# A hybrid decoder layer on one core: squares of two norms summed through PSUM, and a convolution's edge terms on ScalarE

## The chip, the cores and the metric

The kernel runs on one core of a Trainium2 chip. Five engines work beside each other, each on its own queue in order: TensorE (PE; its weight loads are listed apart as PEld), VectorE (DVE), ScalarE (ACT), GpSimd (POOL) and SyncE (SP), which issues most of the DMAs here. The engines work on tiles in SBUF; products land in PSUM, which has eight banks of 128 partitions by 512 floats. The metric is the time of one execution on the device, in microseconds (us).

## The reference, cut to what matters

One decoder layer over a sequence of 1024 positions with 1024 channels, all in float32. Three mixers (a state-space scan, stick-breaking attention, sparse attention) give `mixed`; then comes what the change touches:

```python
def rms_norm(x, w):
    xf = x.astype(jnp.float32)
    y = xf * lax.rsqrt(jnp.mean(xf * xf, axis=-1, keepdims=True) + NORM_EPS)
    return (y * w.astype(jnp.float32)).astype(x.dtype)
...
x = x + rms_norm(mixed @ w_out[l], post_mix_norm[l])
h = rms_norm(x, pre_ffn_norm[l])
u = causal_dwconv(h @ ffn_w_up[l], ffn_conv_w[l], ffn_conv_b[l])
gate, val = jnp.split(u, 2, axis=-1)
f = (jax.nn.gelu(gate, approximate=True) * val) @ ffn_w_down[l]
x = x + rms_norm(f, post_ffn_norm[l])
```

So there is an output projection with a norm behind it, a residual, a second norm, a projection up to 2 x 2816 channels, a causal convolution of three taps along the sequence for each channel, a gate, and a projection down. The convolution of a position needs the two positions before it.

## The kernel before, in words

Tiles are feature major: 128 channels lie on the partitions and 512 positions, half of the sequence, along the free axis. `h` is 0 or 1 for the half. A weight of 128 output channels is one unit. Every product is made of three passes in a reduced format: `load_w` (L263) loads a weight (`wraw`), ACT copies its rounded part (`whi`, L268) and POOL subtracts to get the rest (`wlo`, L269); the input has `hi` and `lo` in the same way, and a product of 128 inputs is hi*hi, hi*lo and lo*hi, recorded at L204. Two buffers hold each of `wraw`, `whi` and `wlo`, so the next weight's split runs while TensorE works on this one.

`tail_stage` (L1199) holds the part around the change. It takes the eight PSUM banks in two pools: `psd` for products (tile `dense`) and `psn` for the norms.

- The output projection runs half by half. For each of eight units, ACT copies the product into `o[j]` (L1303) and `sumsq` squares it with a second activation into an SBUF tile `osq` (L1281), and DVE adds the squares into the first of them (L1285). `rstd` multiplies the sum by a matrix of ones on TensorE, which sums over the partitions, and makes the reciprocal root out of it with DVE and ACT (L1292 to L1297), as a `psn` tile. This product is in full float32, and takes two passes on TensorE.
- Then for each of the eight tiles of the half: scale by the norm (L1310), add the residual `ox` (L1312), square and sum again (L1281, L1285), and write the tile out. `O_POOL` names the tiles, 0 and 2, whose residual addition and whose sum POOL does; these two squares make a sum of their own, so that the second `rstd` has two products with ones to add.
- The second norm scales the tiles (L1318) and splits them into `hi` (ACT, L1321) and `lo` (DVE L1327, or POOL L1325). These are the inputs `h2` of the FFN.
- The first four pairs of FFN units (`N_FIRST`) are computed half by half (`up_half`, L1406). Unit by unit, `conv` (L299) convolves the product: ACT makes the first tap with the bias (L302), DVE keeps the last two columns of the first half (`halo`, L304), adds the shifted taps (L306), and for the second half adds the first columns' terms from the halo (L308). The gate unit goes through Gelu on ACT (L1400), and `gated` multiplies (L1403).
- The other 18 pairs are computed by `up_pair` (L1413): seven products in place of eight from sums and differences of quarters of the weights (`weights7`, L1337: `uf` on POOL L1354 to L1356 and L1359, `uhi` on ACT L1357 and L1360) and of `h2` (`combos`, L1384). Three banks x, y and z of `psd` are in use for a pair; ACT takes copies of partial results (`snap`, L1381), and DVE combines banks and copies (L1421, L1433) before the convolution. One pair is 84 passes on TensorE.
- The down projection (`down`) follows, adding into `acc` in SBUF (L1493), and a last norm.

What order the instructions of an engine have isn't the order of the program: a planner with a simulated time line places them when the program is built, and only calls marked by `keep_in_program_order` stay where they are written. So a change of a few instructions' engines or tiles can reorder others near them. A tile is reused once its readers are done.

## Time and profile before

| what | us |
|---|---|
| median of three runs | 2301.05 (2300.88 to 2301.59) |
| profiled execution | 2302.9 |
| its span | 2300.9 |
| TensorE busy | 2212.4 (96%) |
| VectorE busy | 1399.1 (61%) |
| ScalarE busy | 1126.5 (49%) |
| GpSimd busy | 1112.6 (48%) |

In the profile a row is a group of instructions: line, engine, operation, the tile written and the tiles read, shapes and count, then busy time, mean duration in ns, and the idle time of the engine ahead of them with what ended it. The chain of waits is followed back from the last instruction; it names for each step the work that released the next. The windows give the busy time of the engines in a stretch of the span, and the granted clock of TensorE as a fraction of full speed. In timeline rows the bracket holds the idle time of the engine ahead of the instruction and the instruction that ended it.

### The profile page before, as it was taken

How to read it: one execution, taken by the hardware profiler on the slowest of the kernel's cores; microseconds unless marked ns; L12 is line 12 of the kernel's file. 1: busy time of each engine (PE TensorE's matmuls, PEld its weight loads, DVE VectorE, ACT ScalarE, POOL GpSimd, SP SyncE). 2: the span in 40 equal slices, each digit the busy share in tenths (PEclk: the TensorE clock that was granted, in tenths of full speed). 3: DMA queues.
4: the chain of work that ended last, by engine and by line, in shares of the span. 5: the costliest groups of instructions: out<-in, count | busy, mean ns of one | idle time of the engine just before them, and what ended most of it. 6: DMA issues, size and time to landing. Idle time of an engine off the chain costs nothing.

```text
span 2300.9 us, 29584 instructions
## 1 busy us (share of the span) xinstructions
PE 2212.4 (96%) x10804; PEld 1785.6 (78%) x10804; DVE 1399.1 (61%) x2419; ACT 1126.5 (49%) x1966; POOL 1112.6 (48%) x797
## 2 busy tenths in 40 slices
PE   8999998999999999999999999999899999999997
PEld 7997666667887878887777788887678888878886
DVE  8325784882377667647474543349977777753346
ACT  7144565666466666444444321245545555553224
POOL 4122565566233332635444336446578888822213
PEclk9999999999999999999999999999999999999998
DMA  5223112201111111111212164245322222264312
GB/s 197 80 84 99 53 37 68 65 5 44 47 46 49 48 51 37 65 65 55 74 46 97 68 223 135 94 143 175 107 90 83 83 83 83 83 222 134 93 32 74
DMA packets 102834, 196.57 MB, mean 85 GB/s; under 512 B 26721, under 2 KB 40737, under 8 KB 102689
## 3 DMA queue, kind: packets, MB, share of 16 engines
q1 hardware_dynamic: 102400, 194.47, 25.7%
q8 instruction: 85, 1.39, 0.2%
q14 instruction: 61, 0.49, 0.1%
q10 hardware_dynamic: 288, 0.22, 0.0%
HBM read 150.09 MB, written 44.56 MB: 85 GB/s over the span
## 4 chain that ended last, share of the span: by engine, by line
PE 77%; DVE 15%; issue 3%; ACT 3%; POOL 1%; DMA 1%; SPq 0%; DVEq 0%; ACTq 0%; POOLq 0%
PE dense L204 60%; PE ps_s L204 6%; PE ps_o L204 4%; PE ps_t L204 4%; PE ps_b L204 2%; DVE mx L812 2%; DVE u L306 1%; DVE row L306 1%; DVE x L1312 1%; DVE osq L1285 1%; DMA wraw<-in_wdn 0%; DVE x L1553 0%; POOL wlo L269 0%; DVE x L1465 0%; POOL R L1115 0%
## 5 line engine op out<-in xcount | busy, mean ns | idle before, releaser
L269 POOL TENSOR_TENSOR wlo<-wraw,whi 128x1024 fp32r<-128x1024 f32 (+2 forms) x158 | 327.1, 2071 | 526.1 <-ACT whi L268 516.6
L204 PE MATMUL dense<-h_hi,whi 128*128 128x512 f32 x992 | 401.4, 405 | 3.5 <-DVE row L306 3.4
L204 PE MATMUL dense<-h_lo,whi 128*128 128x512 f32 x992 | 392.9, 396 | 0.0
L204 PE MATMUL dense<-h_hi,wlo 128*128 128x512 f32 x992 | 391.4, 395 | 0.0
L268 ACT ACTIVATE whi<-wraw 128x1024 fp32r<-128x1024 f32 (+2 forms) x158 | 141.4, 895 | 316.9 <-PE dense L204 279.4
L204 PE MATMUL dense<-hi,whi 128*128 128x512 f32 x688 | 268.9, 391 | 3.9 <-ACT whi L268 3.9
L204 PE MATMUL dense<-hi,wlo 128*128 128x512 f32 x688 | 264.4, 394 | 7.1 <-POOL wlo L269 6.5
L204 PE MATMUL dense<-lo,whi 128*128 128x512 f32 x688 | 268.5, 390 | 0.7 <-POOL lo L1325 0.5
L204 PEld LDWEIGHTS dense<-h_hi,whi 128*128 128x128 f32 x992 | 188.1, 190 | 44.5 <-ACT sa L1025 3.6
L204 PEld LDWEIGHTS dense<-h_hi,wlo 128*128 128x128 f32 x992 | 187.5, 189 | 40.2 <-issue 1.1
L204 PEld LDWEIGHTS dense<-h_lo,whi 128*128 128x128 f32 x992 | 188.2, 190 | 36.1 <-issue 1.8
L852 POOL TENSOR_TENSOR wT_lo<-wT,wT_hi 128x512 fp32r<-128x512 f32 x132 | 169.2, 1291 | 90.0 <-ACT wT_hi L851 80.8
L204 PEld LDWEIGHTS dense<-hi,wlo 128*128 128x128 f32 x688 | 129.5, 188 | 36.8 <-POOL wlo L269 8.7
L204 PEld LDWEIGHTS dense<-hi,whi 128*128 128x128 f32 x688 | 129.6, 188 | 33.5 <-ACT whi L268 5.9
L204 PEld LDWEIGHTS dense<-lo,whi 128*128 128x128 f32 x688 | 129.6, 188 | 28.9 <-POOL lo L1325 1.4
L1042 POOL TENSOR_TENSOR s_lo<-sa,s_hi 128x512 fp32r<-128x512 f32 (+2 forms) x48 | 53.7, 1122 | 149.2 <-ACT s_hi L1041 137.8
L204 PE MATMUL dense<-x,uhi 128*128 128x512 f32 x360 | 117.1, 390 | 2.4 <-ACT uhi L1357 1.3
L841 ACT ACTIVATE wT<-ps_s 128x512 f32<-128x512 f32 x132 | 78.5, 594 | 71.1 <-PE ps_s L204 66.4
L306 DVE SCALAR_TENSOR_TENSOR u<-dense,pv,u 128x510 f32<-128x510 f32 (+1 forms) x140 | 101.9, 737 | 6.5 <-ACT u L302 6.4
L812 DVE TENSOR_REDUCE mx<-ps_t 128x1 f32<-128x384 f32 (+3 forms) x192 | 94.0, 514 | 18.8 <-PE ps_t L204 16.7
L1493 DVE TENSOR_TENSOR x<-x,dense 128x512 f32<-128x512 f32 x64 | 43.9, 686 | 86.6 <-PE dense L204 86.6
L851 ACT ACTIVATE wT_hi<-wT 128x512 fp32r<-128x512 f32 x132 | 82.2, 629 | 13.9 <-POOL wT L843 12.1
(422 smaller groups left out, 5271.1 us busy)
## 6 DMA issues: line engine op xcount, KB each, us to landing
wraw<-in_wfm SPq DMA_DIRECT2D x62, 512.0 KB, 3.4
wraw<-in_wup SPq DMA_DIRECT2D x52, 512.0 KB, 3.4
g_d<-gate_e SPq DMA_DIRECT2D x48, 256.0 KB, 2.1
ge<-g_d SPq DMA_DIRECT2D x24, 512.0 KB, 3.8
m_d<-u SPq DMA_DIRECT2D x44, 256.0 KB, 2.0
u<-m_d SPq DMA_DIRECT2D x36, 256.0 KB, 4.3
wraw<-in_wo SPq DMA_DIRECT2D x16, 512.0 KB, 3.4
wraw<-in_wdn SPq DMA_DIRECT2D x32, 256.0 KB, 2.7
```

The source lines that it names most:

```text
L204: i = f(*a, **k)
L268: act(hi, raw, AF.Copy)
L269: (V if tiles else P).tensor_tensor(lo, raw, fl(hi), op=OP.subtract)
L306: V.scalar_tensor_tensor(o[:, d:], ps[:, :512 - d], taps[d], o[:, d:], op0=OP.mult, op1=OP.add)
L812: V.tensor_reduce(mx[:, h, a, n:n + 1], pm[:, :w], axis=AX, op=OP.max)
L841: act(w.rearrange("p h q -> p (h q)"), pz, AF.Exp)
L851: act(hi, wf, AF.Copy)
L852: P.tensor_tensor(lo, wf, fl(hi), op=OP.subtract)
L1042: (P if SB_SLO else V).tensor_tensor(s_lo[:, c0:], a[:, c0:], fl(s_hi[:, c0:]), op=OP.subtract)
L1285: eng.tensor_tensor(sums[0], sums[0], sq, op=OP.add)
L1312: e.tensor_tensor(o[j], o[j], x, op=OP.add)
L1493: end = V.tensor_tensor(a, a, ps, op=OP.add)
```

## The change

Four edits. `sumsq` writes the first square of a norm to an SBUF tile and each later one to a tile of the PSUM pool `psn`; DVE adds it from there. The pool `psn` has three banks in place of two, `psd` five in place of six, and `osq` two buffers in place of six. `O_POOL` is gone: DVE adds all eight residual tiles and all seven sums, and each norm has one product with ones. In the FFN's convolution the first columns of the second half are no longer added by DVE at L308: ACT adds them with three activations of one column (the halo column times the tap, with the output's own column as bias), which are written ahead of DVE's shifted taps. The other convolution, ahead of the scan, keeps its form.

```diff
--- before.py
+++ after.py
@@ -179,13 +179,12 @@
 
 W_BUFS = (3, 4, 4)
 U_BUFS = 4
-OSQ = 6
+OSQ = 2
 
 N_FIRST = 4
 
 SB_SLO = 1
 SB_WLO = 0
-O_POOL = (0, 2)
 H_POOL = (0, 1, 3, 5)
 T_POOL = (range(8), (0, 1, 2))
 
@@ -296,15 +295,19 @@
     def hs(h):
         return slice(h * 512, (h + 1) * 512)
 
-    def conv(o, h, ps, taps, bias, halo):
+    def conv(o, h, ps, taps, bias, halo, by_act=False):
 
         n = len(taps) - 1
         act(o, ps, AF.Identity, bias=bias, scale=taps[0])
+        if h == 1 and by_act:
+            for d in range(1, n + 1):
+                for t in range(d):
+                    act(o[:, t:t + 1], halo[:, n - d + t:n - d + t + 1], AF.Identity, bias=o[:, t:t + 1], scale=taps[d])
         if h == 0:
             V.tensor_copy(halo[:, :n], ps[:, 512 - n:])
         for d in range(1, n + 1):
             V.scalar_tensor_tensor(o[:, d:], ps[:, :512 - d], taps[d], o[:, d:], op0=OP.mult, op1=OP.add)
-            if h == 1:
+            if h == 1 and not by_act:
                 V.scalar_tensor_tensor(o[:, :d], halo[:, n - d:n], taps[d], o[:, :d], op0=OP.mult, op1=OP.add)
 
     st1 = ctx.enter_context(ExitStack())
@@ -1200,8 +1203,8 @@
     E = L(env)
     A, act, V, P, mm, tr, fl, pvc = E.A, E.act, E.V, E.P, E.mm, E.tr, E.fl, E.pvc
     load_w, fm_unit = E.load_w, E.fm_unit
-    psd = es.enter_context(tc.tile_pool(name="psd2", reuse_waits="tile", bufs=6, space=PSUM))
-    psn = es.enter_context(tc.tile_pool(name="psn", reuse_waits="tile", bufs=2, space=PSUM))
+    psd = es.enter_context(tc.tile_pool(name="psd2", reuse_waits="tile", bufs=5, space=PSUM))
+    psn = es.enter_context(tc.tile_pool(name="psn", reuse_waits="tile", bufs=3, space=PSUM))
     mp = es.enter_context(tc.tile_pool(name="mixed", reuse_waits="tile", bufs=1))
 
     def hi_t(dt=R32):
@@ -1275,19 +1278,20 @@
         o = [x_t(F32) for _ in range(8)]
         rows.append(o)
 
-        def sumsq(sums, src, eng=V):
-
-            sq = ow.tile([128, 512], F32, name="osq", bufs=OSQ)
-            act(sq, src, AF.Square)
+        def sumsq(sums, src):
+
             if sums[0] is None:
-                sums[0] = sq
+                sums[0] = ow.tile([128, 512], F32, name="osq", bufs=OSQ)
+                act(sums[0], src, AF.Square)
             else:
-                eng.tensor_tensor(sums[0], sums[0], sq, op=OP.add)
-
-        def rstd(*sums):
+                sq = psn.tile([128, 512], F32, name="psn", tag="psn")
+                act(sq, src, AF.Square)
+                V.tensor_tensor(sums[0], sums[0], sq, op=OP.add)
+
+        def rstd(ss):
+            ss, = ss
             ps = psn.tile([128, 512], F32, name="psn", tag="psn")
-            for n, (ss,) in enumerate(sums):
-                mm(ps, E.ones, ss, start=n == 0, stop=n == len(sums) - 1)
+            mm(ps, E.ones, ss, start=True, stop=True)
 
             V.tensor_scalar(ss, ps, 1.0 / DM, EPS, op0=OP.mult, op1=OP.add)
             act(ps, ps, AF.Ln, scale=1.0 / DM, bias=E.eps)
@@ -1303,16 +1307,15 @@
             act(o[j], ps, AF.Copy)
             sumsq(ss, ps)
         r = rstd(ss)
-        ss, st = [None], [None]
+        ss = [None]
         for j in range(8):
             x = ow.tile([128, 512], F32, name="ox", bufs=8)
             nc.sync.dma_start(x, A["xT"][j * 128:(j + 1) * 128, hs(h)])
             V.scalar_tensor_tensor(o[j], o[j], pvc(PV_PM, j), r, op0=OP.mult, op1=OP.mult)
-            e = P if j in O_POOL else V
-            e.tensor_tensor(o[j], o[j], x, op=OP.add)
-            sumsq(st if j in O_POOL else ss, o[j], e)
+            V.tensor_tensor(o[j], o[j], x, op=OP.add)
+            sumsq(ss, o[j])
             nc.sync.dma_start(E.x1_d[j * 128:(j + 1) * 128, hs(h)], o[j])
-        r = rstd(ss, st)
+        r = rstd(ss)
         for j in range(9):
             if j < 8:
                 i = V.scalar_tensor_tensor(o[j], o[j], pvc(PV_FFN, j), r, op0=OP.mult, op1=OP.mult)
@@ -1395,7 +1398,7 @@
         if h == 0:
             st["halo", s] = up_.tile([128, 4], F32, name="halo", bufs=12)
         st[s, h] = up_.tile([128, 512], F32, name=f"u{s}")
-        E.conv(st[s, h], h, ps, [pvc(PV_FW, 3 * u + 2 - d) for d in range(3)], pvc(PV_FB, u), st["halo", s])
+        E.conv(st[s, h], h, ps, [pvc(PV_FW, 3 * u + 2 - d) for d in range(3)], pvc(PV_FB, u), st["halo", s], True)
         if s == 0:
             act(st[0, h], st[0, h], AF.Gelu_apprx_tanh)
```

## The prediction

> **What bounds the kernel now.** I read the profile from the whole to the place. First the page: busy shares, then the chain that ended last.

> ```profile
> span 2300.9 us, 29584 instructions
> PE 2212.4 (96%) x10804; PEld 1785.6 (78%) x10804; DVE 1399.1 (61%) x2419; ACT 1126.5 (49%) x1966; POOL 1112.6 (48%) x797
> PE 77%; DVE 15%; issue 3%; ACT 3%; POOL 1%; DMA 1%; SPq 0%; DVEq 0%; ACTq 0%; POOLq 0%
> ```

> TensorE is busy 96% of the span. An edit that moves work between the other engines can gain only where TensorE stands still. Where that is, the chain of waits shows by its long unbroken pieces (start, length, work):

> ```profile
> 1301.81 237.31 PE dense L204 x1033
> 1539.12 0.87 PE psn L204 x2
> ...
> 1713.90 285.91 PE dense L204 x1260
> ...
> 2068.93 195.54 PE dense L204 x884
> ```

> Between 1301.8 and 1539.1 us, 1713.9 and 1999.8, and 2068.9 and 2264.5 no edit of DVE, ACT or POOL can gain; it can only lose. One matmul there takes 285.91/1260 = 0.227 us. The changed code runs from 1470 (the output projection) to 2000 (the end of the FFN's up projection), so its chances lie in 1540 to 1714. The windows of that stretch, and one over the FFN loop behind it:

> ```profile
> 1580.00:1600.00 20.00, 18.07 (x77) 14.27 (x77) 18.32 (x23) 11.70 (x17) 13.54 (x7) 1.00 0.35 111
> 1600.00:1620.00 20.00, 18.18 (x78) 14.07 (x77) 19.33 (x23) 9.36 (x15) 9.25 (x4) 1.00 0.58 193
> 1620.00:1640.00 20.00, 17.84 (x75) 13.49 (x74) 16.87 (x26) 15.41 (x21) 13.26 (x7) 1.00 0.37 131
> 1640.00:1660.00 20.00, 14.45 (x55) 10.89 (x54) 20.00 (x32) 9.52 (x15) 9.81 (x3) 0.83 0.20 66
> 1680.00:1700.00 20.00, 17.84 (x77) 13.80 (x76) 18.51 (x12) 10.88 (x17) 18.70 (x9) 1.00 0.19 62
> 1700.00:1720.00 20.00, 16.49 (x72) 13.02 (x71) 9.87 (x19) 9.54 (x14) 13.55 (x10) 1.00 0.25 92
> 1740.00:2000.00 260.00, 260.00 (x1149) 215.29 (x1148) 182.15 (x246) 133.72 (x191) 217.73 (x124) 1.00 0.24 83
> ```

> The columns are the window, its length, then busy time with instructions of TensorE, its weight loads, DVE, ACT and POOL, and the granted clock. TensorE's idle time in the six windows is 1.93 + 1.82 + 2.16 + 5.55 + 2.16 + 3.51 = 17.1 us; that is all the change could take out, 0.74% of the span. In the FFN loop TensorE has none, and DVE is busy 0.70, ACT 0.51, POOL 0.84 of the time. What TensorE waited for from 1500 to 1720:

> ```profile
> PE dense L204 <- POOL wlo L269: 6.3, 3, 4.1
> PE dense L204 <- ACT snap L1381: 3.5, 2, 2.0
> PE dense L204 <- ACT whi L268: 2.6, 3, 1.2
> PE psn L204 <- DVE osq L1285: 1.8, 1, 1.8
> PE dense L204 <- ACT uhi L1357: 1.3, 1, 1.3
> ```

> Only one wait, 1.8 us, is for the sums of squares (osq, L1285). The largest, wlo (L269), is POOL's half of a weight's split; the change doesn't touch it, but it moves the DVE work that holds POOL up:

> ```profile
> 1528.78 2.40 POOL L269 TENSOR_TENSOR wlo<-wraw,whi 128x1024 fp32r<-128x1024 f32 x1 [3.04 <-ACT whi L268]
> 1529.71 2.02 DVE L1285 TENSOR_TENSOR osq<-osq 128x512 f32<-128x512 f32 x1 [3.42 <-ACT osq L1281]
> 1581.75 0.50 PE L204 MATMUL dense<-hi,wlo 128*128 128x512 f32 x1 [1.71 <-POOL wlo L269]
> 1617.91 1.98 PE L204 MATMUL psn<-osq,ones 128*128 128x512 f32 x4 [1.82 <-DVE osq L1285]
> 1642.01 1.89 DVE L1386 TENSOR_TENSOR x<-x 128x512 f32<-128x512 f32 x3
> 1645.11 9.27 POOL L269 TENSOR_TENSOR wlo<-wraw,whi 128x1024 fp32r<-128x1024 f32 x2 [6.03 <-ACT whi L268]
> 1649.24 0.74 DVE L306 SCALAR_TENSOR_TENSOR u<-dense,pv,u 128x511 f32<-128x511 f32 x1
> 1651.58 0.79 PE L204 MATMUL dense<-hi,wlo 128*128 128x512 f32 x1 [4.15 <-POOL wlo L269]
> 1652.17 0.63 PE L204 MATMUL dense<-hi,whi 128*128 128x512 f32 x1
> 1652.60 0.63 PE L204 MATMUL dense<-lo,whi 128*128 128x512 f32 x1
> ```

> An osq sum with both operands in SBUF, issued 0.9 us into a wlo, ends at 1531.73, 0.55 after the wlo: it took 2.02 us. The other way round, two wlo's took 9.27 us from 1645.11 while DVE ran SBUF-only work without a break, against 2.40 each; the first came through only when DVE reached L306 at 1649.24, which reads PSUM. TensorE then stood 4.15 us, and the clock granted in that window was 0.83.

> **The change, part by part.** Prices:

> ```profile
> L1285 DVE TENSOR_TENSOR osq<-osq 128x512 f32<-128x512 f32 x24 | 34.5, 1437 | 29.5 <-ACT osq L1281 28.8
> L1312 DVE TENSOR_TENSOR x<-x,ox 128x512 f32<-128x512 f32 x12 | 14.8, 1287 | 0.0
> L1493 DVE TENSOR_TENSOR x<-x,dense 128x512 f32<-128x512 f32 x64 | 43.9, 686 | 86.6 <-PE dense L204 86.6
> L308 DVE SCALAR_TENSOR_TENSOR u<-halo,pv,u 128x1 f32<-128x1 f32 (+1 forms) x88 | 64.6, 734 | 0.0
> L302 ACT ACTIVATE u<-dense,pv 128x512 f32<-128x512 f32 x70 | 52.1, 769 | 21.8 <-DVE dense L1433 12.1 <-DVE dense L1421 9.1 <-PE dense L204 0.5
> L1381 ACT ACTIVATE snap<-dense 128x512 f32<-128x512 f32 x72 | 40.2, 584 | 2.8 <-PE dense L204 2.8
> L974 ACT ACTIVATE row<-dense 128x4 fp32r<-128x4 f32 x16 | 2.8, 172 | 4.9 <-DVE row L971 3.9 <-DVE row L975 0.9
> ```

> (1) Squares through PSUM. DVE's 24 sums of 1437 ns become 28 sums with one operand in PSUM, which I price like L1493, also DVE with one operand in PSUM: 0.69. DVE goes from 34.5 to 19.3 us, and these sums leave POOL's way. It hides almost wholly: in 1500 to 1540 TensorE doesn't wait. Only the four norms' chains can show it. POOL loses four x additions and two osq sums; DVE gains four additions at 1.29 (L1312), 5.2 us, which here lie between the two norms of a half, ahead of the sum the next norm needs.

> (2) One sum instead of two in the second norm. A ones product is two passes in the trace ("x4" for two products at 1617.91, 1.98 us). Two products go, one per half; the chain's "PE psn" at 1539.12 prices one product, two passes, at 0.87. TensorE: 2 × 0.87 = −1.7 us, since those passes stand among products that TensorE runs without a gap.

> (3) One PSUM bank less for the products (six to five), one more for squares. A pair of the FFN loop is 84 products, 19.05 us at 0.227. Following the banks through TensorE's order, a bank is written again at the earliest 29 products (6.6 us) after its last write, in place of 39 (8.8 us). What must be over by then is the subtraction and the convolution that read the bank. In the loop:

> ```profile
> 1771.35 0.70 DVE L1433 TENSOR_TENSOR dense<-dense,snap 128x512 f32<-128x512 f32 x1 [0.80 <-PE dense L204]
> ...
> 1774.44 0.74 DVE L306 SCALAR_TENSOR_TENSOR u<-dense,pv,u 128x510 f32<-128x510 f32 x1
> ```

> From z's last product to the last read of its bank, 1771.35 to 1775.18, are 3.8 us; 6.6 − 3.8 = 2.8 us are left. Cost nothing; if that cover is gone, each of 18 pairs pays what is over.

> (4) Convolution terms of the second half: 88 L308 of DVE (64.6 us) become 132 activations of one column. Lower bound 0.172 (L974); upper bound 0.172 plus what scale and bias from a tile add to a 512-wide copy, 0.769 − 0.584 = 0.185, so 0.36. I take 0.36, as these have both operands: 132 × 0.36 = 48 us for ACT, six per pair, 2.1 of 19.05 us; ACT would go from 0.51 to 0.62. Ends: 23 and 48 us of ACT. In the loop that is hidden by TensorE's gapless run. But the DVE terms of such a unit now start after ACT's third, about 1.1 us behind the Identity (L302), and DVE saves 0.73 twice: the release of the bank moves by about −0.4 us. Uncovered, it would cost up to 1.1 us on a pair.
> [...]

> **Where it shows.** I placed the instructions in the new order on each engine and carried the durations above forward from 1540. Changes of TensorE's time:
> - First half, 1540 to 1600. The eight x additions on DVE end about where they did; the second norm's sums end 2 us earlier (0.69 in place of stretched ones). But the norm's Exp now sits on ACT behind a weight copy and a square that wait for TensorE, so r comes 0.5 us later. The copies of the weights move ahead of the copies of h2, which takes out the 1.71 at 1581.75; the first two up units are interleaved in the new order, hold both weight buffers and wait again for 0.5 and 0.9. Net about −0.5.
> - Second half, 1600 to 1640. The 1.82 at 1617.91 goes. In its place one wlo is late by about 2.0, as its whi is queued on ACT behind a square, a table load and a Gelu. Net +0.2.
> - 1640 to 1660. DVE's run of SBUF-only work ahead of the first L306 grows from 13 instructions to 15 (0.6 us each, as they start in a row): wlo comes 1.2 later. Net +1.2.
> - 1660 to 1714. The L308 before the first pairs are gone from DVE: uhi 0.45, and the second snap, behind the Gelu behind DVE, some 0.9 earlier. Net −1.3.
> - The loop, the down projection and the tail: 0; the order of their products is the same but for bank reuse.

> Sum: −1.7 − 0.5 + 0.2 + 1.2 − 1.3 = −2.1 us. The profiled execution took 2302.9 (its span and 2.0 around it), 1.85 over the median of the three runs, 2301.05. So: 2302.9 − 2.1 = 2300.8 by its own measure, 2298.9 by the median's.

> The unknown ends: each of the four place terms is a difference of queue positions, and is at best its whole wait gone (1.9, 1.8, 4.15, 3.5), at worst as much again.

> **The rivals.**
> (a) The loop breaks (slower). The three column terms stand on ACT between the Identity and everything queued behind it, the next uhi and snap among them, and z's bank has 6.6 us to come free. For: ACT waits in order. Against: ACT is idle half of the loop. It decides when the release takes over 6.6 us. With 0.4 us on each of 18 pairs, 7.2: 2298.9 + 7.2 = 2306.
> (b) The waits of both norms and POOL's fall away (faster). If DVE no longer meets POOL, then 1.71, 1.82 and most of the 4.15 go, with the half-rate products behind it (eight at 0.43 by their starts, +0.2 each, 1.6): 1.7 + 1.9 + 1.8 + 3 + 1 = 9.4 at best, 2292. For: the stretched rows. Against: the SBUF-only run at 1641 to 1649 is the combos' (L1386 to L1388), which the change doesn't touch.
> (c) ACT's order turns against it (slower). More activations stand in a row ahead of whi, and a late whi makes wlo late. If the wlo wait of the second half is 4 in place of 2, with a drop of the clock as at 1651.58, +2 + 1.6, and the same once more in the first half: 2298.9 + 5 = 2304.
> The clock's price is in the rows after 1651.58: 0.43 between starts instead of 0.227. [...]
> (d) Nothing but the saved product: 2301.05 − 1.7 = 2299.4, inside the forecast's own range.

> **How the numbers follow.** A measurement of this kernel tells 0.2% (4.6 us) from no change. Forecast with (d), 2296.4 to 2303: 0.46. (b), 2290 to 2296.4: 0.30. (a) 0.10 and (c) 0.14, together 2303 to 2311. Nearly all of the forecast's case is within 0.2% (0.42 of 0.46, the rest 0.02 on either side); of (b) nine tenths (0.27) are faster by more, of (a) and (c) seven tenths (0.17) slower by more. So faster 0.29, slower 0.19, same 0.52. The range leaves out the best of (b) and the worst of (a): 2291.5 to 2306.5.

> **What would show it.** L1285 at 0.69, 28 times, with psn as an operand; psn products two rows per norm; the new activations at 0.17 to 0.36, 132 times; no L308 on u; a TensorE piece of about 286 us again in the chain (a broken one is rival a); the waits for wlo within 1640 to 1660 near 5.4 (near 1: rival b; a second above 3: rival c). I am wrong if the loop isn't gapless, if the 1.2 at 1651 has the other sign, or if stages ahead of 1500 or behind 2000 differ by over 2 us.

## The result and the profile after

The changed kernel takes 2305.65 us in the median of 17 executions (2300.04 to 2307.67), the kernel before 2300.88 beside it (2299.47 to 2302.76): a ratio of 1.0016, with a 95% interval of 1.0010 to 1.0023. It is slower: by 3.7 us by the ratio, by 4.8 between these medians. Forecast was 2298.9, 2.1 less than before; the time is inside the stated range (2291.5 to 2306.5) and inside 0.2%, but on the other side of no change.

From the page of the changed kernel, and the long pieces of its chain of waits:

```profile
span 2303.9 us, 29654 instructions
PE 2216.0 (96%) x10800; PEld 1790.1 (78%) x10800; DVE 1341.3 (58%) x2339; ACT 1163.6 (51%) x2098; POOL 1102.4 (48%) x791
PE 80%; DVE 12%; ACT 3%; issue 2%; POOL 2%; DMA 1%; DVEq 0%; ACTq 0%; POOLq 0%
```

```profile
1302.18 236.90 PE dense L203 x1033
...
1699.34 299.74 PE dense L203 x1314
...
2064.90 202.56 PE dense L203 x908
```

TensorE has four rows less (10800 for 10804: two products with ones) and is yet busy 3.6 us longer, 2216.0 for 2212.4. The FFN loop runs unbroken, up to 1999.08 us where it ended at 1999.81 before, so at that point the changed kernel is 0.7 us ahead. The groups of instructions show that the column terms (0.376 us) and the sums (0.684) cost what was forecast, 0.36 and 0.69; the residual additions came cheaper, 0.818 where 1.29 was taken:

```profile
L305 ACT ACTIVATE u<-halo,u,pv 128x1 f32<-128x1 f32 x132 | 43.4, 376 | 0.6
L1289 DVE TENSOR_TENSOR osq<-osq,psn 128x512 f32<-128x512 f32 x28 | 19.1, 684 | 43.4 <-ACT psn L1288 42.7
L1315 DVE TENSOR_TENSOR x<-x,ox 128x512 f32<-128x512 f32 x16 | 12.1, 818 | 0.0
```

What TensorE waited for from 1500 us to the end, the largest sums (total, times, longest):

```profile
PE dense L203 <- POOL wlo L268: 7.7, 5, 5.4
PE psn L203 <- ACT u L1545: 6.8, 2, 4.3
PE dense L203 <- ACT whi L267: 5.8, 5, 2.8
PE dense L203 <- DVE u L309: 2.6, 1, 2.6
PE dense L203 <- ACT uhi L1363: 2.4, 2, 2.2
```

New is a wait for DVE's convolution (L309). The waits for snaps (L1381 of before) are gone, and of the one for osq (L1285 of before) 0.24 us are left. And the windows, with the granted clock in the last column but two:

```profile
1640.00:1660.00 20.00, 13.20 (x43) 9.67 (x42) 16.72 (x23) 9.84 (x18) 11.96 (x3) 0.74 0.19 66
1680.00:1700.00 20.00, 14.87 (x62) 11.00 (x61) 17.52 (x14) 12.82 (x24) 19.24 (x9) 1.00 0.25 82
1700.00:1720.00 20.00, 20.00 (x83) 16.42 (x82) 6.24 (x13) 9.78 (x17) 14.57 (x9) 0.92 0.19 64
1720.00:2000.00 280.00, 280.00 (x1237) 231.94 (x1236) 169.03 (x204) 168.55 (x293) 232.15 (x135) 1.00 0.24 83
2000.00:2070.00 70.00, 64.86 (x269) 52.35 (x269) 40.70 (x53) 41.44 (x77) 27.69 (x17) 0.95 0.57 203
```

The kernel before, over the last of these windows:

```profile
2000.00:2070.00 70.00, 65.22 (x285) 52.72 (x284) 41.10 (x62) 36.81 (x60) 28.40 (x18) 1.00 0.55 189
```

The same 70 us hold 269 products after and 285 before, though TensorE is busy for nearly the same time, 64.9 and 65.2. The clock is the difference: 0.95 for 1.00. Timeline rows of TensorE in the changed kernel behind its four long waits (the bracket is the wait):

```profile
1649.34 0.79 PE L203 MATMUL dense<-hi,wlo 128*128 128x512 f32 x1 [5.41 <-POOL wlo L268]
...
1699.34 0.50 PE L203 MATMUL dense<-hi,whi 128*128 128x512 f32 x1 [2.55 <-DVE u L309]
1699.67 0.48 PE L203 MATMUL dense<-lo,whi 128*128 128x512 f32 x1
1699.95 0.63 PE L203 MATMUL dense<-hi,wlo 128*128 128x512 f32 x1
1700.38 0.63 PE L203 MATMUL dense<-hi,whi 128*128 128x512 f32 x1
...
2026.20 0.73 PE L203 MATMUL dense<-x,uhi 128*128 128x512 f32 x2 [2.20 <-ACT uhi L1363]
2063.54 0.50 PE L203 MATMUL dense<-hi,whi 128*128 128x512 f32 x1 [2.77 <-ACT whi L267]
```

Behind each of the four, products start 0.43 us apart for a time, in place of 0.227 (half rate, in what follows; the granted clock is 0.50 from 1649.34 to 1655.40). I count steps of 0.40 to 0.46 us between `dense` products after 1300 us: 34 in the changed kernel, 6 in the one before (behind its 4.15 us wait). 28 of them at 0.2 us are 5.6 us. The waits of over 0.4 us from 1300 to 2270 add up to 20.1 us after and 20.8 before. With the 1.7 us of the two products gone that makes, as an estimate, −0.7 − 1.7 + 5.6 = 3.2, and the spans differ by 3.0. So in these two executions the waits together are no longer than before; they are fewer and each is longer, and the clock falls behind more of them.

### The profile page after: what moved, and what is told of

It is laid out like the page before. It is cut to its first block, busy times and chain, and to the rows that moved or that the text cites. A ratio compares the mean times of both kernels' runs of the same rounds, so it can differ in the third digit from the quotient of the medians.

```text
span 2303.9 us, 29654 instructions
## 1 busy us (share of the span) xinstructions
PE 2216.0 (96%) x10800; PEld 1790.1 (78%) x10800; DVE 1341.3 (58%) x2339; ACT 1163.6 (51%) x2098; POOL 1102.4 (48%) x791
## 4 chain that ended last, share of the span: by engine, by line
PE 80%; DVE 12%; ACT 3%; issue 2%; POOL 2%; DMA 1%; DVEq 0%; ACTq 0%; POOLq 0%
PE dense L203 63%; PE ps_s L203 6%; PE ps_o L203 4%; PE ps_t L203 4%; PE ps_b L203 2%; DVE mx L815 2%; POOL wlo L268 1%; DVE row L309 1%; DVE x L1468 1%; DVE u L309 0%; DMA wraw<-in_wdn 0%; DVE x L1556 0%; ACT whi L267 0%; POOL R L1118 0%; DMA x<-m_d 0%
## 5 line engine op out<-in xcount | busy, mean ns | idle before, releaser
L268 POOL TENSOR_TENSOR wlo<-wraw,whi 128x1024 fp32r<-128x1024 f32 (+2 forms) x158 | 328.0, 2077 | 545.1 <-ACT whi L267 516.2
L203 PEld LDWEIGHTS dense<-h_hi,wlo 128*128 128x128 f32 x992 | 187.4, 189 | 40.2 <-issue 1.1
L309 DVE SCALAR_TENSOR_TENSOR u<-dense,pv,u 128x510 f32<-128x510 f32 (+1 forms) x140 | 102.3, 743 | 10.2 <-ACT u L305 8.3
L815 DVE TENSOR_REDUCE mx<-ps_t 128x1 f32<-128x384 f32 (+3 forms) x192 | 94.0, 514 | 18.4 <-PE ps_t L203 16.3
L1496 DVE TENSOR_TENSOR x<-x,dense 128x512 f32<-128x512 f32 x64 | 43.9, 687 | 86.7 <-PE dense L203 86.6
L854 ACT ACTIVATE wT_hi<-wT 128x512 fp32r<-128x512 f32 x132 | 82.2, 629 | 13.8 <-POOL wT L846 12.1
```

The source lines that it names most:

```text
L203: i = f(*a, **k)
L268: (V if tiles else P).tensor_tensor(lo, raw, fl(hi), op=OP.subtract)
L309: V.scalar_tensor_tensor(o[:, d:], ps[:, :512 - d], taps[d], o[:, d:], op0=OP.mult, op1=OP.add)
L815: V.tensor_reduce(mx[:, h, a, n:n + 1], pm[:, :w], axis=AX, op=OP.max)
L854: act(hi, wf, AF.Copy)
L1496: end = V.tensor_tensor(a, a, ps, op=OP.add)
```

## The experiments

Theories at the start: A, that the loss is this clock, and that the column terms on ACT make the waits that it follows; B, that it is made in the norms. C, D and those that follow are told with their runs. Each run has its kernel before on the same chip beside it.

**The two halves of the change, the banks, and the same kernel again.** First the convolution back on DVE:

```diff
-        E.conv(..., st["halo", s], True)
+        E.conv(..., st["halo", s])
```

> The changed kernel, with the convolution's first columns of the second half back on DVE (L308's work as before); squares, banks and residual additions as changed. Theory A (the loss comes through the granted clock: the column terms on ACT make waits of 2.2 to 2.8 us at 1699, 2026 and 2063, each followed by some 9 products at half rate, 26 x 0.2 = 5.3 us): those drops are gone, one drop of some 14 products near 1650 stays, and the time is 2298 to 2301, at or under before. Rival B (the loss is made in the output projection and the norms, by the wait for wlo that grew from 4.15 to 5.41 and its half-rate products): it stays slower, 2303 to 2306.

2303.41 us, beside 2301.05; ratio 1.0008 (0.9999 to 1.0016). Theory A as put has failed: without the column terms on ACT the kernel isn't at 2298 to 2301, and its profile has a wait of 7.05 us for the convolution at 1698, longer than the 2.55 with them. B named the time, but not the cause: the norms as before don't take the loss away, as the run of the banks alone will show.

Then the column terms alone, in the kernel before:

```diff
+        if h == 1 and by_act:
+            ... act(o[:, t:t + 1], halo[...], AF.Identity, bias=o[:, t:t + 1], scale=taps[d])
...
+        E.conv(..., st["halo", s], True)
```

> The kernel before, with only the convolution's column terms moved to ACT. Theory A: slower than before, 2303 to 2306, with more products at half rate behind the waits near 1700, 2026 and 2063, and executions that differ among themselves by more than those of before. Rival B: within 1.5 us of before, as the norms are unchanged.

2299.24 us, ratio 0.9992 (0.9983 to 1.0001). Not slower, and if anything faster. Its executions lie closer together (2298.07 to 2300.95) than those of before; that part of A failed too.

Then the changed kernel with the pools as before:

```diff
-    psd = ... bufs=5
-    psn = ... bufs=3
+    psd = ... bufs=6
+    psn = ... bufs=2
```

> The changed kernel with six banks for the products and two for squares and norms, as before. Rival C (the fifth bank is what TensorE misses, at 1699 above all, where it waits 2.55 us for the convolution's last read of a bank): that wait is gone with its drop, 2300 to 2303. Theory A without C: that wait has another name but stays over 2 us, and the time is 2304 to 2307 as changed.

2300.34 us, ratio 0.9994 (0.9985 to 1.0003): the loss is gone. So it hangs on the banks, as C says. The wait for the convolution is gone from its profile, but TensorE now waits 4.7 us at 1632 for the `hi` of the normalized tiles. The planner orders this kernel's instructions otherwise than the changed kernel's from about 1553 us on, so this run alone doesn't tell the banks from the new order.

> The changed kernel once more, for a second profile and its executions on the chip and in the hour of the other three. [...] Rival D (the executions differ by their DMAs): the waits themselves differ, the half-rate products don't.

2303.16 us, ratio 1.0015 (1.0006 to 1.0023), as in the first comparison. The second profile has nearly the same waits and other half-rate products, where D has it the other way round. Its row for the wait for the convolution, the two that follow, and the one wait that differs by more than 0.1 us (2.77 in the first profile, for a weight's `whi`):

```profile
1697.02 0.50 PE L203 MATMUL dense<-hi,whi 128*128 128x512 f32 x1 [2.54 <-DVE u L309]
1697.36 0.40 PE L203 MATMUL dense<-lo,whi 128*128 128x512 f32 x1
1697.59 0.39 PE L203 MATMUL dense<-hi,wlo 128*128 128x512 f32 x1
...
2060.66 0.50 PE L203 MATMUL dense<-hi,whi 128*128 128x512 f32 x1 [3.85 <-ACT whi L267]
```

After the same wait (2.54 and 2.55) products follow at 0.23 here and at 0.43 in the first profile. This profile has 19 half-rate steps for 34, and a span of 2300.6 for 2303.9: 15 steps at 0.2 are 3.0 us, where the spans differ by 3.3 (the second is besides 1.0 ahead at 1592 already, and loses 1.1 by the longer wait). So the same wait of the same kernel is followed by half rate in one execution and not in another. Over all 28 executions of the changed kernel the time goes with the mean granted clock: 2306.8 in the mean at 0.985 (5 executions), 2305.8 at 0.986 (11), 2303.3 at 0.987 (5), 2301.1 at 0.988 (6), and one more at 0.989. The kernel before has 2301.3 at 0.988 (39 of 94 executions) and 2298.0 at 0.990 (12). At 0.988 the two kernels are alike; the changed one is there less often. (Some of that clock is lost during the waits themselves: in the first profile it is 0.50 from 1645.3 to 1649.3, where TensorE stands. So this alone doesn't separate wait and clock; the wait at 1699 in the two profiles does.)

**The banks alone, and what the waits are worth.** The kernel before with nothing changed but the pools:

```diff
-    psd = ... bufs=6
-    psn = ... bufs=2
+    psd = ... bufs=5
+    psn = ... bufs=3
```

> The kernel before with the pool sizes alone changed: five banks for the products, three for the norms. Theory E (the changed pools make the loss: with five banks the products that open the FFN's pairs, near 1699, wait for a bank that a late convolution still reads): slower than before, 2302 to 2305, with a wait near 1700 that names DVE's convolution (L306 or L308) and is over 2 us. Rival F (the move of POOL's additions and sums to DVE makes it): within 1 us of before.

2306.99 us, ratio 1.0031 (1.0019 to 1.0042). Theory E holds, with a loss above the 2302 to 2305 that it gave, and F falls: two numbers make the whole loss, and more. Up to 1722 us the two profiles have the same order of operations on all four engines, so what differs at 1700 is no doing of the planner. What TensorE waited for most from 1500 to 2100 us in this kernel, and DVE's timeline ahead of the first wait with the product that waited:

```profile
PE dense L204 <- DVE u L306: 7.0, 1, 7.0
PE dense L204 <- POOL wlo L269: 6.5, 4, 4.2
PE dense L204 <- ACT uhi L1360: 3.2, 2, 3.0
```

```profile
1682.08 6.89 DVE L1465 TENSOR_TENSOR x<-x,hi 128x512 fp32r<-128x512 f32 x4
1688.89 10.05 DVE L1465 TENSOR_TENSOR x<-x,lo 128x512 fp32r<-128x512 f32 x4
1698.86 0.74 DVE L306 SCALAR_TENSOR_TENSOR u<-dense,pv,u 128x511 f32<-128x511 f32 x1
1699.52 0.20 DVE L308 SCALAR_TENSOR_TENSOR u<-halo,pv,u 128x1 f32<-128x1 f32 x1
1699.65 0.74 DVE L306 SCALAR_TENSOR_TENSOR u<-dense,pv,u 128x510 f32<-128x510 f32 x1
...
1700.44 0.80 PE L204 MATMUL dense<-hi,whi 128*128 128x512 f32 x1 [7.04 <-DVE u L306]
```

The L306 at 1698.86 to 1700.39 convolves the last unit of the half-by-half stage. On DVE it stands behind eight L1465, which take 17 us; the last four of them 2.5 each (10.05 together), where VectorE's additions of the same shape took 0.63 (three in 1.89 at 1642 before). POOL is busy 18.4 us of the 20 from 1680 to 1700 here, and idle at 1642 before (from 1639.1 to 1645.1). The kernel before has the same train, and its convolution is as late, yet there the product of that place runs at 1694.97 without a wait:

```profile
1694.97 0.39 PE L204 MATMUL dense<-hi,whi 128*128 128x512 f32 x1
1697.91 2.87 DVE L1465 TENSOR_TENSOR x<-x,lo 128x512 fp32r<-128x512 f32 x1
1700.71 0.74 DVE L306 SCALAR_TENSOR_TENSOR u<-dense,pv,u 128x511 f32<-128x511 f32 x1
```

With six banks TensorE has a free one for the second product of the next pair, and only later waits for snaps (2.02 and 1.49). With five, that product needs the bank which the late convolution reads. With the column terms on ACT this wait is 2.55 in place of 7.05. That isn't why the full change is better than the banks alone: the changed kernel without the column terms has the whole wait, 7.05, and stands no worse (1.0008 beside 1.0015).

Next, products of constants by ones into a bank that nobody reads, where TensorE waits for wlo at 1645:

```diff
...
+                        if k == 0 and a is lo:
+                            fill(7)      # 7 x mm(psn tile, E.ones, E.tab[:, :512])
```

> The changed kernel with seven products of constants by ones in a bank that nobody reads, put on TensorE where it waits 5.4 us for wlo near 1645; they add work (7 x 0.86 = 6.0 us of it) and no result depends on them. Theory A (half rate behind a wait costs 6 to 13 products x 0.2 us there): the wait shrinks to under 1 us, no product behind it is at half rate, and the time falls by 1 to 2.5 us from the changed kernel's, to 2301 to 2302.5, with the granted clock up by about 0.001. If half rate doesn't come of standing still, the time stays or rises by what the added work is too long.

2305.57 us, ratio 1.0016 (1.0006 to 1.0025), where the changed kernel had 1.0015 in the batch before. The wait fell from 5.41 to 0.55 and its half rate went, as expected, but not the time. TensorE comes earlier to the wait for the convolution, and stands there 5.90 us:

```profile
1699.61 0.79 PE L203 MATMUL dense<-hi,whi 128*128 128x512 f32 x1 [5.90 <-DVE u L309]
```

It goes on at 1699.61, and in the changed kernel at 1699.34. So in this profile what was won at 1645 was lost again at 1700, where the end of DVE's train sets when TensorE goes on. The train ended no earlier though DVE came to it 2 us earlier: its first two instructions (one row here) took 4.66 us, where the changed kernel's (second and third row) took 0.70 and 0.84.

```profile
1679.38 4.66 DVE L1489 TENSOR_TENSOR x<-x,hi 128x512 fp32r<-128x512 f32 x2 [3.45 <-ACT hi L1488]
1681.47 0.70 DVE L1468 TENSOR_TENSOR x<-x,hi 128x512 fp32r<-128x512 f32 x1 [3.45 <-ACT hi L1467]
1683.04 0.84 DVE L1468 TENSOR_TENSOR x<-x,hi 128x512 fp32r<-128x512 f32 x1 [0.86 <-ACT hi L1467]
```

The same wait taken away at its cause, with two wlo's on VectorE:

```diff
-        (V if tiles else P).tensor_tensor(lo, raw, fl(hi), op=OP.subtract)
+        (V if tiles or on_v else P).tensor_tensor(lo, raw, fl(hi), op=OP.subtract)
...
+            load_w(A["wup"][u], 1024, on_v=h == 1 and f == 1)
```

> The changed kernel with the wlo of the two units that wait longest (the second pair of units of the second half) made by VectorE in its own order, in place of POOL that VectorE's SBUF-only work holds up. Theory G (POOL's wlo is held up by VectorE; 2.4 us of work took 7.7): the wait of 5.4 falls to about 2, and with the half rate behind it the time falls by 4 to 5 us, to 2298 to 2300. Rival H (wlo is late because its whi is late on ACT): the wait stays at 4 or more and the time within 1.5 us of the changed kernel's.

2302.99 us, ratio 1.0013 (1.0004 to 1.0022). The wait fell from 5.41 to 2.48, so it was POOL held up (G), not a late whi (H). Half rate still follows it, though, and the 4 to 5 us didn't come. Here the gain does pass the wait at 1700: that wait is as long as it was (2.54), and TensorE goes on from it at 1695.46, 3.9 us earlier than in the first profile of the changed kernel and 1.6 earlier than in the second. Why the median hardly moved isn't shown; its interval is about 2 us to either side.

> The kernel before with the convolution's column terms on ACT, and the same two wlo's on VectorE. By theory G the column terms alone, 2299.2, lose the 5.4 us wait and its half rate: 2294 to 2296, faster than both kernels by more than 0.2%. By rival H 2298 to 2300.

2298.65 us, ratio 0.9988 (0.9979 to 0.9996): the fastest in ratio, under both kernels, but by 0.12%, not the 0.2% and more that G had promised. Its time is one that H gave, though the wait fell to 2.51, as G says; half rate follows that wait here too.

**The order on VectorE, and a wait with nothing behind it.** The train is broken, with the last four L1465 held behind the last convolution:

```diff
-        V.tensor_tensor(lo, t, fl(hi), op=OP.subtract)
+        if q == 4:
+            with tc.issue_after(first[-1]["end", 1].ins):
+                V.tensor_tensor(lo, t, fl(hi), op=OP.subtract)
+        else: ...
```

> The kernel before with five banks and three, and VectorE's last four lo's for the first pair (L1465, those of its fourth product) held behind the last convolution of the half-by-half units. Theory E, made exact (TensorE waits 7.0 us at 1700 because the fifth bank, the one it needs next, is read by a convolution that stands on VectorE behind eight L1465): the wait at 1700 falls to under 2 us, and the time by 4 to 7 us from five and three banks alone (2307.0), to 2300 to 2303. Rival I (the wait has another cause, such as the snaps on ACT): it stays over 4 us.

2303.84 us, ratio 1.0010 (1.0001 to 1.0019), beside 1.0031 without the hold. The wait for L306 is gone. Of the time 3.2 us came back between the medians, and 4.8 by the ratios, which are each taken beside the kernel before of their hour; the time is just over the 2300 to 2303 expected, and a new wait stands behind the old one. The largest waits of TensorE from 1500 to 2100 us there:

```profile
PE dense L204 <- POOL wlo L269: 6.5, 4, 4.2
PE dense L204 <- ACT snap L1381: 4.2, 1, 4.2
PE dense L204 <- ACT uhi L1360: 3.1, 2, 2.9
```

> The changed kernel with the same hold. By theory E its wait of 2.5 us at 1699 goes with its half rate: 2 to 4 us under the changed kernel's, 2300 to 2303. By rival I unchanged.

2302.71 us, ratio 1.0005 (0.9996 to 1.0014). The wait for L309 went here too, and one of 3.33 us for a snap came at 1705; its profile shows 21 half-rate steps. The median points the way of E, inside the noise.

> Six banks and two as before, squares as before, the column terms on ACT, the two wlo's of the second pair of units on VectorE and the same hold: what the runs so far speak for. Without the hold 2298.7. By theory E the convolution comes earlier here too, but with six banks TensorE doesn't wait for it: 2296 to 2299, faster than both kernels.

2299.64 us, ratio 0.9989 (0.9980 to 0.9998), no better than without the hold, under the kernel before by 0.11%, and just over the 2296 to 2299 that were expected.

Last, three such constant products ahead of the fifth unit of the down projection, behind which TensorE runs without a gap for 200 us in the changed kernel:

```diff
+            if ci == 0 and j == 4:
+                fill(3)
...
```

The lines left out here, and in the run with seven such products, keep products of the unit itself in program order.

> The changed kernel with three products of constants by ones (2.6 us of added work that no result depends on) on TensorE ahead of the fifth unit of the down projection, where it waits 2.7 to 3.9 us for a weight's DMA and then runs without a gap to the tail. Theory A: no half rate behind that wait, 5 to 9 products x 0.2 us, so 1 to 1.8 us under the changed kernel's time in the same hour, though the work is added. If half rate has nothing to do with the wait, the time is equal or longer.

2303.24 us, ratio 1.0008 (0.9999 to 1.0017). In its profile the wait is 0.62 us, and the products behind it keep full rate:

```profile
2058.76 0.50 PE L203 MATMUL dense<-hi,wlo 128*128 128x512 f32 x1 [0.62 <-POOL wlo L268]
2059.09 0.39 PE L203 MATMUL dense<-hi,whi 128*128 128x512 f32 x1
```

The place does what A says. But the executions range from 2298.39 to 2310.10, and their median can't tell a gain of 1 to 1.8 us from none; this stays open in the time.

## Why the prediction was wrong

**(1) Squares through PSUM: right.** 28 sums of 0.684 (0.69 forecast), and of the norm's wait of 1.82 us 0.24 are left. With five and three banks, the squares and DVE's additions bring the time from 2306.99 to 2303.41 (two batches). With six and two the whole change stands at 0.9994 and the column terms alone at 0.9992: nothing to be seen of the squares' gain. That it is lost to squares that wait for one of two psn banks is argued, not shown.

**(2) One product instead of two: right.** Four rows less, 0.86 for each product that stays.

**(3) The banks: wrong, and the step that failed.** "Cost nothing" was worked out from the loop, where bank reuse was said to leave 2.8 us, and the loop has in fact no wait. But the reuse that decides, with the pools alone changed, is at the loop's entrance, where one convolution stands behind eight stretched L1465. The late convolution was in the trace of before, hidden by the sixth bank; I looked at the tightest distance in products, and not at each reader's place on DVE. Alone it costs 6.3 us (2306.99 against 2300.65); in the changed kernel it makes the difference of 1.0015 to 0.9994, some 5 us.

Where the five banks cost in the changed kernel is another matter. TensorE's lead (−) or lag (+) in us against the profile of the kernel before, once the same number of its products is left to run (the columns are times in the profile of before):

| profile | 1692 | 1715 | 1998 | 2060 | 2075 |
|---|---|---|---|---|---|
| pools alone | −1.7 | +3.5 | +4.0 | +5.8 | +4.3 |
| changed kernel, first | −0.6 | −0.3 | −0.3 | 0.0 | +3.0 |
| changed kernel, second | −2.9 | −4.2 | −4.2 | −4.0 | −0.3 |

With the pools alone changed, the 5.2 us are lost at 1700. The changed kernel loses next to nothing there, as the kernel before waits for snaps where this one waits for the convolution. It loses 3.0 and 3.7 us at one place of the down projection, where TensorE waits 2.77 and 3.85 us for a weight and then runs at half rate for a time; the kernel before waits 1.33 there, at full rate. So the forecast's "the loop, the down projection and the tail: 0" failed as well, and its own sign of being wrong, a stage behind 2000 that differs by over 2 us, came. The five profiles with five banks and the column terms and no products added there wait 2.68 to 3.85 us at that place, all others at most 1.33; why these two together make the wait stays open.

**(4) Column terms on ACT: right in price and cover.** 0.376 each, where 0.36 was taken, and the loop unbroken: rival (a) didn't come. Alone they stand at 0.9992 (0.9983 to 1.0001), which doesn't tell a gain from none. Beside five banks they shorten the wait at 1700 from 7.05 to 2.55, and the time is no shorter for it (2303.41 without them, 2303.16 with them).

**The places.** The wait for wlo at 1650 was forecast at 5.4 and is 5.41, behind a run of 15 SBUF-only instructions on DVE, as forecast; the runs show that it comes with the column terms (15 and 5.41 us with them alone, 12 and 3.60 with all but them). The psn wait of 1.8 went, as said. The first of the four place terms foresaw waits of 0.5 and 0.9 for weights, and one of 0.52 came. The second took 2.0 for a wlo that came with 1.33. The fourth term, −1.3 for 1660 to 1714, has the wrong sign at its core: the two snap waits went (3.5) and 2.55 came with some 8 slow products.

**The clock, the other half.** The prediction priced a wait by its length, except at 4.15. In the profile of before the waits of 1.71 and 1.82 are followed by full rate: dense products start 0.23 apart from 1582.09, and the four ones passes at 1617.91 take 1.98 us. Rival (c) had the drop, at a wlo wait of 4 us; that wait is 1.33, and that its 2304, like the 2306 of rival (a), lies near the measured time is luck. (Its sum is wrong as well: 2 + 1.6 twice is 7.2, not 5, which makes 2306.) The runs showed it behind shorter waits than that: of the waits of dense products in the 14 profiles, 10 of the 14 from 2.0 to 2.6 us and none of the 104 under 1.6 (counted from 0.4) were followed by half rate. One of 2.81 was not. That is where the 3.0 us of the first profile are: ahead by 0.7 at 1999 (0.3 by the number of products), then in 2000 to 2070 waits of 5.1 in place of 4.8, and some 16 half-rate products, 3.3 us. **Not settled**: how much of the median is clock and how much wait. The runs show that the pools make the loss. That the order on DVE at 1700 is its place, they show for the pools alone; in the changed kernel the profiles put it behind the loop, and the medians of the runs that take away the one wait or the other (2302.71 and 2303.24) can't decide.

## What to carry to other kernels

When a pool loses a buffer, look for the latest reader of any of its buffers, first of all where one stage hands over to the next; the steady loop's slack says nothing of its entrance. A wait taken away ahead of a later one can be worth nothing, as with the seven constant products: ask what the engine will wait for next. And count waits by length, not by sum: from 1300 to 2270 us, 14 waits of 20.8 us in all came with 6 half-rate steps in the kernel before, 12 of 20.1 with 34 in the changed one.

## What the runs showed of the hardware

- In the kernel with the pools alone changed, half rate came behind a wait of 1.83 us: the four passes of the ones products behind the osq wait start 0.85 apart (3.61 us for the four), where they start 0.43 apart in the kernel before, behind 1.82 (1.98 us). The granted clock from 1600 to 1620 is 0.91 there, and 1.00 before.

```profile
1615.64 3.61 PE L204 MATMUL psn<-osq,ones 128*128 128x512 f32 x4 [1.83 <-DVE osq L1285]
```
